# Attention scores with low parts of the keys stored twice, all matmuls over 128 rows

## The chip, the cores and the metric

The kernel runs on one core of a Trainium2 chip. The metric is the time of one execution on the device, in microseconds (us). TensorE (PE) multiplies matrices, VectorE (DVE), ScalarE (ACT) and GpSimd (POOL) work on tiles in the on-chip memory, and SyncE (SP) issues the DMA transfers, one after the other in a fixed order.

## The reference

Two transformer-like blocks over 1024 tokens of 1024 features, all in float32; the first block has two layers, each an attention mixer and a convolutional gated feed-forward. Only the mixer matters here. It runs four groups of four heads and adds their projections:

```python
o_a = neighbourhood_attention_2d(a_q, a_k, a_v, na_rpb[l])     # A: a window of 8 x 16 grid points, with a bias
o_b = dense_attention_blocked(q_b, k_b, v_b, 96 ** -0.5)       # B: latent keys, 96 wide
o_c = dense_attention_blocked(q_c, k_c, c_v, 64 ** -0.5)       # C: two key heads for four query heads
o_d = sliding_window_sink_attention(q_d, k_d, d_v, sink, ...)  # D: +-128 tokens, two key heads
mixed = jnp.concatenate([o_a, o_b, o_c, o_d], axis=-1) @ w_out[l]
```

In A, C and D a score is the product of a query and a key of 64 elements.

## The kernel before

Float32 accuracy is had from float32r matmuls: every operand x is split into h (rounded to float32r) and l = x - h, and a product is h\*h + h\*l + l\*h. For the heads of 64 elements the three products are packed into two matmuls, in `fused` (L561 to L564): the query tile holds h in one half of its 128 rows and l in the other, the tile kh holds the keys' h twice below each other, so that the first matmul (L563) gives h\*h + l\*h; the second (L564) adds h\*l from the 64 rows that hold the query's h, against a tile kl that holds the low parts of two key heads below each other.

```python
nc.tensor.matmul(ps, lhsT=q, rhs=kh, start=True, stop=False)
nc.tensor.matmul(ps, lhsT=q[b], rhs=kl[b], start=False, stop=True)
```

For the first key head of a pair q is [h; l], for the second [l; h], since h must stand in the rows of that head's kl. Three attentions use `fused`:

- C (`c_scores`): 4 heads x 8 query tiles, blocks of 1024 keys, two 512-column pairs each. Its queries (`cqs`), keys (`ckh`) and low parts (`ckl`) are laid into tiles by DMA moves (`cq_dests`, `k_dests`) that SP issues before the attention.
- D (`d_block`): 4 heads x 8 tiles, one pair of 256 or 384 columns. Operands were spilled to memory (`dq_dests`, `k_dests`) and are loaded again (`dq`, `dk`); the mask `dmask` is added.
- A (`a_block_of`): 2 pairs of heads x 8 tiles, one pair of 512 columns or of 512 and 128. `a_qk` spills its operands, `a_load` loads 5 operand tiles for a pair of heads, and two bias images a head: 896 columns for the first and last two query tiles, 640 for the four in the middle.

After a block's scores come a row maximum on VectorE (L555, L585 or L616), the exponential on ScalarE (L557, L587, L618), transposes on TensorE (L510), their split (L515 to L517) and the products with the values (L533, L527).

Projections (`a_qk`, `a_v`, `d_q`, `b_latent` and others) run beside the attentions as a queue of steps (`Feed`); six steps of it come ahead of C. A planner reorders the instructions of each engine from the program's order when the kernel is built, by estimated costs; the buffers of a tag are taken in program order (`fifo`). The tag q has 10 buffers of [128, 1024], which hold all operands above and the biases; the tag pj has 8 of [128, 512]. In PSUM the tag A, which takes the scores, has two buffers of 1024 columns. A move is one DMA (`move`, L350); a weight is loaded by L210 and split by L241 and L242.

Of the kernel before, what the change touches and what calls it, by code (L numbers as in the profile page):

```python
# [50 lines left out]
# spilled operands of the first block's attention: tiles of [128, 1024]  # L51
P_DQ, P_DK, P_AV, P_A, P_BV, P_KPE, P_N = 0, 4, 7, 11, 21, 25, 26


def run(gen):
    """runs a generator to its end and returns what it returns"""
    while True:
        try:
            next(gen)
        except StopIteration as e:  # L60
            return e.value
# [5 lines left out]
class Feed:  # L67
    """work in steps, to be emitted between the steps of other work"""
# [29 lines left out]
class Net:  # L98
# [39 lines left out]
    def fifo(self):  # L138
        """buffers of a tag are taken in program order"""
# [18 lines left out]
    def t(self, tag, dt=F32):  # L158
        """a buffer of a tag: [128, 1024] or [128, 512]"""
# [6 lines left out]
    def ps(self, tag):  # L166
        """A: two banks; T, O, J: one bank"""
# [26 lines left out]
    # ---- weights: load a 128 x n image, split it into two float32r parts  # L194
# [3 lines left out]
    def weights(self, srcs, n):  # L198
        """images beside each other, n columns in all"""
# [17 lines left out]
    def weight_x(self, src, k):  # L217
        """a weight image of k x 512 columns, split into buffers of the tag x"""
# [10 lines left out]
    def mm3(self, ps, terms, first=True, last=True):  # L229
        """terms: ((stationary h, l), (moving h, l)) pairs summed into ps"""  # L230
# [7 lines left out]
    def split(self, full, h, l, eng=None):  # L238
        """h = float32r(full), l = full - h"""
# [22 lines left out]
    def mean_sq(self, tiles, width, tag="v", fast=False):  # L262
        """mean over the features (partitions of all tiles) of the squares, on every partition; fast: no sums on VectorE, the first few on GpSimd"""
# [26 lines left out]
    # ---- x (8 tiles of [128 features, 512 tokens]) -> split normalised x  # L290
# [32 lines left out]
    # ---- x_new = x_old + rms(y) * gain, in y's place  # L323
# [14 lines left out]
    # ---- feature-major projection of a weight tile, half by half  # L338
# [13 lines left out]
    # ================================================================ mixing  # L352
    def mix(self, l, xs, src, dst):
# [16 lines left out]
        # ---- rotary embedding of two tiles that hold the halves of every head  # L370
# [39 lines left out]
        # query heads as [h; l] for the first key head and [l; h] for the second  # L410
        def cq_dests(ah, al, bh, bl):
            for h in range(4):
                r = slice(32 * h, 32 * h + 32)
                for k, s in enumerate((ah, bh, al, bl) if h < 2 else (al, bl, ah, bh)):
                    self.move(cqs[h][32 * k:32 * k + 32], s[r])

        def dq_dests(ah, al, bh, bl):
            for h in range(4):
                r = slice(32 * h, 32 * h + 32)
                for k, s in enumerate((ah, bh, al, bl) if h < 2 else (al, bl, ah, bh)):  # L420
                    self.move(PR[P_DQ + h, 32 * k:32 * k + 32], s[r])

        def k_dests(ah, al, bh, bl):
            for h in range(2):
                for k, (sh, so) in enumerate(((ah, al), (bh, bl))):
                    c, d = slice(32 * h, 32 * h + 32), slice(64 + 32 * h, 96 + 32 * h)
                    r = slice(64 * h + 32 * k, 64 * h + 32 * k + 32)
                    for r0 in (32 * k, 64 + 32 * k):
                        self.move(ckh[h][r0:r0 + 32], sh[c])
                        self.move(PR[P_DK + h, r0:r0 + 32], sh[d])  # L430
                    self.move(ckl[r], so[c])
                    self.move(PR[P_DK + 2, r], so[d])

        # ---- token-major values of 128 tokens: [128, 4 heads x (h | l)], h,l for even heads and l,h for odd
# [24 lines left out]
        # ---- attention  # L459
        def combine(o, s, chunk, q0, narrow):  # L460
            direct = chunk in (0, 3)
            """rows of the even head: h part + l part; of the odd head: l part + h part; over the sums"""
# [24 lines left out]
        def products(o, e, V, vh, P, s, chunk, qq):  # L487
            """adds the products of the values with the transposed exponentials of some query tiles"""
# [51 lines left out]
        def attend(pair, quarters, block, V, vh, chunk):  # L540
            """block(e, head, query tile, sum) -> (exponentials [128, keys], first key tile, number of key tiles)"""
# [19 lines left out]
        def fused(ps, q, b, kh, kl):  # L561
            """q = [h; l] or [l; h], kh twice below each other, kl in the rows b of q's h"""
            nc.tensor.matmul(ps, lhsT=q, rhs=kh, start=True, stop=False)  # L563
            nc.tensor.matmul(ps, lhsT=q[b], rhs=kl[b], start=False, stop=True)  # L564
# [3 lines left out]
        def c_scores(ps, h, q0):  # L568
            for c in (slice(0, 512), slice(512, 1024)):
                fused(ps[:, c], cqs[h][:, q0:q0 + 128], rows(h // 2), ckh[h // 2][:, c], ckl[:, c])  # L570

        def d_block(e, h, i, s):
# [6 lines left out]
            fused(ps, dq[h][:, i * 128:i * 128 + 128], rows(h // 2), dk[h // 2][:, kc], dk[2][:, kc])  # L579
# [10 lines left out]
        def a_load(n):  # L590
            """operands and biases of a pair of neighbourhood heads"""
            ops = [load(P_A + 5 * n + k) for k in range(5)]
            G = []
            for e in range(2):
                g, gm = self.t("q"), self.t("q")
# [1212 lines left out]
```

## Time and profile before

| | |
|---|---|
| median of 3 runs | 3912.29 us (3910.96 to 3913.23) |
| profiled execution, span from first to last instruction | 3919.4 us |
| TensorE matmuls, busy | 3678.4 us (94%), 17088 matmuls |
| VectorE, busy | 2399.7 us (61%) |
| ScalarE, busy | 1614.8 us (41%) |
| GpSimd, busy | 1576.9 us (40%) |
| mean granted clock of TensorE | 0.967 |

The profile is of one execution, another than the three runs; the page gives its span and no separate time for it. Times inside the trace count from the first instruction. TensorE's matmuls overlap (a row's duration goes on while the next has started), so its pace is read from the distance of starts. In the forms of TensorE's rows, "64\*128" is a stationary operand of 64 rows and 128 columns and "64x512" the moving one. "issue" as a releaser means that the profile shows nothing that the engine waited for. SPq rows are DMA issues by SP. A row of busy time by stretch gives the stretch and its length, then the busy time and, in brackets, the instructions of PE, PEld (weight loads), DVE, ACT and POOL, then the granted clock, the DMA share and GB/s.

### The profile page before, as it was taken

The page shows a single profiled execution, that of the slowest core. Times are in us where ns is not written, and L with a number is a line of the kernel's source. Part 1 is how long each engine was busy: PE and PEld are TensorE (multiplying, and loading weights), DVE is VectorE, ACT ScalarE, POOL GpSimd, SP SyncE. Part 2 cuts the span into 40 slices and gives each one's busy share as a digit, 9 for nine tenths or more (in the row PEclk, how much of TensorE's full clock was granted, in tenths as well). Part 3 has the DMA queues.
Part 4 walks back from the last instruction along what each step waited for, and adds up shares of the span by engine and source line. Part 5 has one row for each costly group of instructions (what it writes and reads, how often), then busy time and mean ns, then how long its engine had stood idle before and what let it go on. Part 6 is the DMA issues. An engine that isn't in the chain of part 4 may idle for free. (4 is left out here: it accounts for less than half of the span.)

```text
span 3919.4 us, 46844 instructions
## 1 busy us (share of the span) xinstructions
PE 3678.4 (94%) x17088; PEld 2936.3 (75%) x17088; DVE 2399.7 (61%) x3218; ACT 1614.8 (41%) x2802; POOL 1576.9 (40%) x1176
## 2 busy tenths in 40 slices
PE   6999999899999998999999979999999889897998
PEld 5777678678888885767677858888887668776776
DVE  6465865865564437556775784344534878686547
ACT  4344755433222233345665544234443433324333
POOL 4344433632222224534533463222323454545444
PEclk9999999899999998999999989999999989998999
DMA  3532553322222113343364432111111311111114
GB/s 105 144 105 98 177 170 133 104 100 84 78 81 84 49 57 116 92 120 121 105 204 126 137 108 68 62 54 52 62 60 60 113 49 54 43 49 38 52 52 142
DMA packets 201752, 362.99 MB, mean 93 GB/s; under 512 B 26289, under 2 KB 49073, under 8 KB 201521
## 3 DMA queue, kind: packets, MB, share of 16 engines
q1 hardware_dynamic: 201520, 360.00, 29.0%
q8 instruction: 134, 2.20, 0.2%
q14 instruction: 98, 0.79, 0.1%
HBM read 268.14 MB, written 73.93 MB: 87 GB/s over the span
## 5 line engine op out<-in xcount | busy, mean ns | idle before, releaser
L242 POOL TENSOR_TENSOR wlZ<-wrZ,whZ 128x512 fp32r<-128x512 f32 x584 | 823.7, 1428 | 1512.1 <-ACT whZ L241 1431.1
L235 PE MATMUL AZ<-xZ,whZ 128*128 128x512 f32 x4096 | 1280.7, 393 | 32.4 <-DVE pZ L1416 13.0
L235 PEld LDWEIGHTS AZ<-xZ,whZ 128*128 128x128 f32 x4096 | 773.2, 189 | 203.0 <-issue 18.2
L235 PE MATMUL AZ<-xZ,wlZ 128*128 128x512 f32 x2048 | 803.2, 392 | 3.8 <-POOL wlZ L242 3.4
L241 ACT CAST whZ<-wrZ 128x512 fp32r<-128x512 f32 x584 | 335.2, 613 | 959.5 <-issue 343.6
L235 PEld LDWEIGHTS AZ<-xZ,wlZ 128*128 128x128 f32 x2048 | 387.5, 189 | 88.0 <-POOL wlZ L242 6.0
L980 DVE SCALAR_TENSOR_TENSOR vZ<-AZ,pv,vZ 128x1023 f32<-128x1023 f32 x168 | 215.1, 1280 | 342.7 <-ACT vZ L975 340.2
L517 POOL TENSOR_TENSOR ptZ<-pfZ,ptZ 128x512 fp32r<-128x512 f32 (+1 forms) x200 | 263.9, 1320 | 347.6 <-DVE ptZ L516 316.2
L235 PE MATMUL JZ<-xZ,whZ 128*128 128x512 f32 (+1 forms) x1120 | 369.7, 406 | 33.8 <-DVE xZ L242 7.8
L515 ACT COPY pfZ<-TZ 128x512 f32<-128x512 f32 (+2 forms) x400 | 219.7, 557 | 261.2 <-PE TZ L510 168.8
L235 PE MATMUL TZ<-qZ,whZ 128*128 128x512 f32 x856 | 266.9, 393 | 22.3 <-DVE pjZ L1365 14.9
L533 PE MATMUL OZ<-ptZ,vZ 128*128 128x256 f32 (+1 forms) x1344 | 262.2, 310 | 23.5 <-POOL ptZ L517 11.2
L516 DVE CAST ptZ<-pfZ 128x512 fp32r<-128x512 f32 (+2 forms) x400 | 206.2, 520 | 125.0 <-ACT pfZ L515 120.2
L235 PEld LDWEIGHTS JZ<-xZ,whZ 128*128 128x128 f32 (+1 forms) x1120 | 203.7, 189 | 87.4 <-issue 10.2
L510 PE MATMUL TZ<-ident,pZ 128*128 128x128 f32 x1488 | 243.4, 285 | 18.5 <-ACT pfZ L515 12.6
L533 PEld LDWEIGHTS OZ<-ptZ,vZ 128*128 128x128 f32 x1344 | 201.2, 198 | 48.0 <-POOL ptZ L517 14.1
L235 PE MATMUL JZ<-xZ,wlZ 128*128 128x512 f32 (+1 forms) x560 | 223.7, 399 | 0.9 <-POOL wlZ L242 0.9
L510 PEld LDWEIGHTS TZ<-ident,pZ 128*128 128x128 f32 x1488 | 179.5, 145 | 50.7 <-ACT pfZ L515 18.7
L555 DVE TENSOR_REDUCE s1Z<-AZ 128x1 f32<-128x1024 f32 x128 | 156.3, 1222 | 89.8 <-PE AZ L564 48.3
L235 PEld LDWEIGHTS TZ<-qZ,whZ 128*128 128x128 f32 x856 | 161.7, 190 | 58.5 <-issue 15.7
L1392 DVE SCALAR_TENSOR_TENSOR vZ<-qZ,pv,vZ 128x1009 f32<-128x1009 f32 (+14 forms) x120 | 193.4, 1630 | 4.1 <-ACT vZ L1382 2.4
L235 PE MATMUL TZ<-qZ,wlZ 128*128 128x512 f32 x428 | 167.8, 394 | 0.0
(434 smaller groups left out, 6213.0 us busy)
## 6 DMA issues: line engine op xcount, KB each, us to landing
wrZ<-wup SPq DMA_DIRECT2D x184, 256.0 KB, 2.8
wrZ<-wi SPq DMA_DIRECT2D x156, 256.0 KB, 2.8
wrZ<-wdn SPq DMA_DIRECT2D x112, 256.0 KB, 2.8
qZ<-sc_pr SPq DMA_DIRECT2D x34, 512.0 KB, 4.4
wrZ<-wo SPq DMA_DIRECT2D x64, 256.0 KB, 2.8
sc_ot<-cbZ SPq DMA_DIRECT2D x56, 256.0 KB, 2.5
xZ<-sc_ot SPq DMA_DIRECT2D x56, 256.0 KB, 5.4
wrZ<-modw SPq DMA_DIRECT2D x48, 256.0 KB, 2.8
```

Of the source, the lines that this page charges most:

```text
L235: self.nc.tensor.matmul(ps, lhsT=a, rhs=b, start=first and k == 0, stop=last and k == n - 1)
L241: nc.scalar.copy(h, full)
L242: (eng or nc.vector).tensor_tensor(out=l, in0=full, in1=h.bitcast(F32), op=ALU.subtract)
L510: nc.tensor.transpose(ps[:, n:n + 128], blk, self.ident)
L515: nc.scalar.copy(pf[:, 0:n], ps[:, 0:n])
L516: nc.vector.tensor_copy(ph[:, 0:n], pf[:, 0:n])
L517: (nc.gpsimd if SHARE[self.turn2 % len(SHARE)] else nc.vector).tensor_tensor(out=pl[:, 0:n], in0=pf[:, 0:n], in1=ph[:, 0:n].bitcast(F32), ...
L533: nc.tensor.matmul(o[:, c0:c0 + w], lhsT=v, rhs=x[:, at[k]:at[k] + w], start=(k == order[0] and x is ph), stop=(k == order[-1] and x is pl ...
L555: nc.vector.tensor_reduce(out=nmx, in_=ps, axis=AX.X, op=ALU.max, negate=True)
L980: nc.vector.scalar_tensor_tensor(out=o, in0=i, scalar=w, in1=o, op0=ALU.mult, op1=ALU.add)
L1392: nc.vector.scalar_tensor_tensor(out=o, in0=i, scalar=w[k], in1=o, op0=ALU.mult, op1=ALU.add)
```

## The change

The low parts of the keys get a tile for each key head, in which they stand twice below each other like the high parts; the query tile is [h; l] for every head; the second matmul takes all 128 rows, and so also adds l\*l. The spilled operands grow (`P_DK` 3 to 4 tiles, `P_A` 5 to 6 for a pair of heads). `k_dests` makes 32 moves instead of 24, `a_qk` 8 instead of 5 for each half of a key projection. The bias of A is loaded in three parts of 640 columns: for the first two query tiles, for the middle four, and, when query tile 2 of the first head comes, for the last two. The mask of D goes from a q buffer to a pj buffer. Comments and texts in the functions were taken out as well.

```diff
-P_DQ, P_DK, P_AV, P_A, P_BV, P_KPE, P_N = 0, 4, 7, 11, 21, 25, 26
+P_DQ, P_DK, P_AV, P_A, P_BV, P_KPE, P_N = 0, 4, 8, 12, 24, 28, 29
...
-                for k, s in enumerate((ah, bh, al, bl) if h < 2 else (al, bl, ah, bh)):
+                for k, s in enumerate((ah, bh, al, bl)):
...
         def k_dests(ah, al, bh, bl):
-            for h in range(2):
-                for k, (sh, so) in enumerate(((ah, al), (bh, bl))):
-                    c, d = slice(32 * h, 32 * h + 32), slice(64 + 32 * h, 96 + 32 * h)
-                    r = slice(64 * h + 32 * k, 64 * h + 32 * k + 32)
-                    for r0 in (32 * k, 64 + 32 * k):
-                        self.move(ckh[h][r0:r0 + 32], sh[c])
-                        self.move(PR[P_DK + h, r0:r0 + 32], sh[d])
-                    self.move(ckl[r], so[c])
-                    self.move(PR[P_DK + 2, r], so[d])
+            for part, (tiles, pr, srcs) in enumerate(((ckh, P_DK, (ah, bh)), (ckl, P_DK + 2, (al, bl)))):
+                for h in range(2):
+                    for k, src in enumerate(srcs):
+                        for r0 in (32 * k, 64 + 32 * k):
+                            self.move(tiles[h][r0:r0 + 32], src[32 * h:32 * h + 32])
+                            self.move(PR[pr + h, r0:r0 + 32], src[64 + 32 * h:96 + 32 * h])
...
-        def fused(ps, q, b, kh, kl):
+        def fused(ps, q, kh, kl):
             nc.tensor.matmul(ps, lhsT=q, rhs=kh, start=True, stop=False)
-            nc.tensor.matmul(ps, lhsT=q[b], rhs=kl[b], start=False, stop=True)
+            nc.tensor.matmul(ps, lhsT=q, rhs=kl, start=False, stop=True)
...
-                fused(ps[:, c], cqs[h][:, q0:q0 + 128], rows(h // 2), ckh[h // 2][:, c], ckl[:, c])
+                fused(ps[:, c], cqs[h][:, q0:q0 + 128], ckh[h // 2][:, c], ckl[h // 2][:, c])
...
-            ops = [load(P_A + 5 * n + k) for k in range(5)]
-            G = []
-            for e in range(2):
-                g, gm = self.t("q"), self.t("q")
-                nc.sync.dma_start(g[:, 0:896], I["rpbx"][l, 2 * n + e, :, 0:896])
-                nc.sync.dma_start(gm[:, 0:640], I["rpbx"][l, 2 * n + e, :, 896:1536])
-                G.append((g, gm))
-            return ops, G
+            ops = [load(P_A + 6 * n + k) for k in range(6)]
+            G = {}
+
+            def bias(part):
+                for e in range(2):
+                    G[part, e] = self.t("q")
+                    c = (256, 896, 0)[part]
+                    nc.sync.dma_start(G[part, e][:, 0:640], I["rpbx"][l, 2 * n + e, :, c:c + 640])
+
+            bias(0)
+            bias(1)
+            return ops, G, bias
...
             def a_block(e, h, i, s):
                 nk, k0 = NA_NK[i] * 128, NA_KS[i] * 64
+                if i == 2 and e == 0:
+                    load_bias(2)
...
                         for e in range(2):
                             for r in range(2):
-                                self.move(PR[P_A + 5 * n + 2 + e, rows(r), sl], h[rows(e)])
-                        self.move(PR[P_A + 5 * n + 4, :, sl], lo)
+                                self.move(PR[P_A + 6 * n + 2 + e, rows(r), sl], h[rows(e)])
+                                self.move(PR[P_A + 6 * n + 4 + e, rows(r), sl], lo[rows(e)])
...
-        ckl = self.t("q", F32R)
+        ckl = [self.t("q", F32R) for _ in range(2)]
...
-        dmask = self.t("q")[:, 0:384]
+        dmask = self.t("pj")[:, 0:384]
...
-        dk = [load(P_DK + h) for h in range(3)]
+        dk = [load(P_DK + h) for h in range(4)]
```

## Rows read from the trace of the kernel before

**Rows 1.** Busy time by stretch: C, D, A of layer one; both layers' sum.
```profile
150.00:332.00 182.00, 178.44 (x962) 135.31 (x961) 113.88 (x164) 88.23 (x170) 71.84 (x56) 0.98 0.38 115
332.00:432.00 100.00, 94.49 (x520) 68.69 (x520) 72.61 (x168) 60.32 (x153) 52.75 (x68) 0.97 0.32 104
432.00:532.00 100.00, 95.94 (x490) 70.34 (x489) 76.16 (x183) 62.98 (x148) 38.03 (x35) 0.92 0.63 196
...
sum 751.00, PE 725.03 PEld 540.38 DVE 522.26 ACT 421.04 POOL 323.89; mean PE 120.84 PEld 90.06 DVE 87.04 ACT 70.17 POOL 53.98
```
**Rows 2.** Waits of VectorE, 150 to 332 us: total, times, longest.
```profile
DVE s1Z L555 <- PE AZ L564: 23.9, 21, 2.7
```

**Rows 3.** Busy time by stretch, around the end of D.
```profile
400.00:450.00 50.00, 44.39 (x228) 29.26 (x227) 45.55 (x106) 37.34 (x94) 30.98 (x35) 0.93 0.41 133
```

**Rows 4.** Timeline of TensorE's matmuls in C: start, duration, line, forms, count.
```profile
200.47 0.40 PE L563 MATMUL AZ<-qZ,qZ 128*128 128x512 f32 x1
200.79 0.50 PE L564 MATMUL AZ<-qZ,qZ 64*128 64x512 f32 x1
201.22 0.50 PE L563 MATMUL AZ<-qZ,qZ 128*128 128x512 f32 x1
...
202.08 0.33 PE L510 MATMUL TZ<-ident,pZ 128*128 128x128 f32 x1
...
204.55 0.62 PE L235 MATMUL JZ<-xZ,whZ 128*128 128x512 f32 x2
205.01 0.40 PE L235 MATMUL JZ<-xZ,wlZ 128*128 128x512 f32 x1
```

**Rows 5.** Line L564: instructions, and idle time of its engine before them.
```profile
L564 PE MATMUL AZ<-qZ,qZ x288: 322/492/792, 150.7 to 2054.2; 64*128 64x512 f32 x110, 64*128 64x384 f32 x22, 64*128 64x256 f32 x12
...
  issue: 59.6, 239
```

**Rows 6.** Timeline of TensorE's matmuls in attention B.
```profile
559.16 1.55 PE L235 MATMUL AZ<-xZ,qZ 96*128 96x512 f32 x6
560.54 0.52 PE L533 MATMUL OZ<-ptZ,vZ 128*128 128x256 f32 x3
```

**Rows 7.** Timeline of TensorE in D: two pairs, between the first and last row.
```profile
385.54 0.42 PE L563 MATMUL AZ<-qZ,qZ 128*128 128x384 f32 x1
...
387.00 0.57 PE L527 MATMUL OZ<-ptZ,vZ 128*64 128x128 f32 x6
```

**Rows 8.** Timeline of TensorE in D, where one pair is interleaved.
```profile
352.82 0.34 PE L563 MATMUL AZ<-qZ,qZ 128*128 128x384 f32 x1
353.00 0.49 PE L510 MATMUL TZ<-ident,pZ 128*128 128x128 f32 x3
...
354.26 0.44 PE L564 MATMUL AZ<-qZ,qZ 64*128 64x384 f32 x2
354.63 0.50 PE L235 MATMUL JZ<-xZ,whZ 128*128 128x512 f32 x1
```

**Rows 9.** Timeline of TensorE in A: transposes, then a block of 640 columns.
```profile
452.15 0.66 PE L510 MATMUL TZ<-ident,pZ 128*128 128x128 f32 x4
452.57 0.37 PE L533 MATMUL OZ<-ptZ,vZ 128*128 128x256 f32 x1
...
454.18 0.47 PE L563 MATMUL AZ<-qZ,qZ 128*128 128x512 f32 x1
...
455.52 0.50 PE L563 MATMUL AZ<-qZ,qZ 128*128 128x512 f32 x1
```

**Rows 10.** Busy time by stretch, in the first 15 us of C.
```profile
161.00:164.00 3.00, 3.00 (x8) 1.45 (x6) 1.12 (x2) 2.28 (x4) 1.28 (x1) 0.50 0.89 230
```

**Rows 11.** Timeline of TensorE at the start of C; idle time and releaser in brackets.
```profile
158.49 0.44 PE L510 MATMUL TZ<-ident,pZ 128*128 128x128 f32 x2 [1.83 <-ACT pZ L557]
```

**Rows 12.** Timeline of SP's DMA issues at the start of C, layer one.
```profile
136.71 0.54 SPq L350 DMA_DIRECT2D qZ<-qZ  x1
...
151.01 15.11 SPq L350 DMA_DIRECT2D sc_pr<-pjZ  x22
166.17 1.55 SPq L210 DMA_DIRECT2D wrZ<-wi  x3
```

**Rows 13.** Timeline of ScalarE at the start of C, layer one.
```profile
154.74 0.60 ACT L653 ACTIVATE pjZ<-TZ 128x512 fp32r<-128x512 f32 x1 [9.02 <-DMA sc_pr<-pjZ]
```

**Rows 14.** Timeline of ScalarE at the start of C, layer two.
```profile
1683.78 0.60 ACT L653 ACTIVATE pjZ<-TZ 128x512 fp32r<-128x512 f32 x1 [10.01 <-DMA sc_pr<-pjZ]
```

More of the change, by code (lines that the diff above doesn't have):

```diff
@@ L419, in dq_dests @@
                 r = slice(32 * h, 32 * h + 32)
-                for k, s in enumerate((ah, bh, al, bl) if h < 2 else (al, bl, ah, bh)):
+                for k, s in enumerate((ah, bh, al, bl)):
                     self.move(PR[P_DQ + h, 32 * k:32 * k + 32], s[r])
         def k_dests(ah, al, bh, bl):
-            for h in range(2):
-                for k, (sh, so) in enumerate(((ah, al), (bh, bl))):
-                    c, d = slice(32 * h, 32 * h + 32), slice(64 + 32 * h, 96 + 32 * h)
-                    r = slice(64 * h + 32 * k, 64 * h + 32 * k + 32)
-                    for r0 in (32 * k, 64 + 32 * k):
-                        self.move(ckh[h][r0:r0 + 32], sh[c])
-                        self.move(PR[P_DK + h, r0:r0 + 32], sh[d])
-                    self.move(ckl[r], so[c])
-                    self.move(PR[P_DK + 2, r], so[d])
+            for part, (tiles, pr, srcs) in enumerate(((ckh, P_DK, (ah, bh)), (ckl, P_DK + 2, (al, bl)))):
[4 more added lines that the diff above has]
+                            self.move(PR[pr + h, r0:r0 + 32], src[64 + 32 * h:96 + 32 * h])
         def v_tile(ps, dst):
@@ L578, in d_block @@
             kc = slice(k0 * 128, k0 * 128 + n)
-            fused(ps, dq[h][:, i * 128:i * 128 + 128], rows(h // 2), dk[h // 2][:, kc], dk[2][:, kc])
+            fused(ps, dq[h][:, i * 128:i * 128 + 128], dk[h // 2][:, kc], dk[2 + h // 2][:, kc])
             sink = self.nsink[:, l * 4 + h:l * 4 + h + 1]
@@ L590, in a_load, with a_block_of @@
         def a_load(n):
-            ops = [load(P_A + 5 * n + k) for k in range(5)]
-            G = []
-            for e in range(2):
-                g, gm = self.t("q"), self.t("q")
-                nc.sync.dma_start(g[:, 0:896], I["rpbx"][l, 2 * n + e, :, 0:896])
-                nc.sync.dma_start(gm[:, 0:640], I["rpbx"][l, 2 * n + e, :, 896:1536])
-                G.append((g, gm))
-            return ops, G
-        def a_block_of(ops, G):
+            ops = [load(P_A + 6 * n + k) for k in range(6)]
[8 more added lines that the diff above has]
+            return ops, G, bias
+        def a_block_of(ops, G, load_bias):
             def a_block(e, h, i, s):
                 nk, k0 = NA_NK[i] * 128, NA_KS[i] * 64
+                if i == 2 and e == 0:
+                    load_bias(2)
                 ps = self.ps("A")
@@ L606, in a_block @@
                     c1 = min(nk, c0 + 512)
-                    fused(ps[:, c0:c1], ops[e][:, i * 128:i * 128 + 128], rows(e),
-                          ops[2 + e][:, k0 + c0:k0 + c1], ops[4][:, k0 + c0:k0 + c1])
-                if 2 <= i <= 5:
-                    bias = G[e][1][:, 0:640]
-                else:
-                    o = (NA_KS[i] - 2 * i + 6) * 64
-                    bias = G[e][0][:, o:o + nk]
+                    fused(ps[:, c0:c1], ops[e][:, i * 128:i * 128 + 128],
+                          ops[2 + e][:, k0 + c0:k0 + c1], ops[4 + e][:, k0 + c0:k0 + c1])
+                part = 0 if i < 2 else 1 if i < 6 else 2
+                o = 0 if part == 1 else (NA_KS[i] - 2 * i + 6) * 64 - (256, 0, 0)[part]
+                bias = G[part, e][:, o:o + nk]
                 p = self.t("p")
@@ L654, in a_qk @@
                         nc.vector.scalar_tensor_tensor(out=lo, in0=ps, scalar=sc, in1=h.bitcast(F32), op0=ALU.mult, op1=ALU.subtract)
-                        for e, hl in enumerate(((h, lo), (lo, h))):
-                            for r in range(2):
-                                self.move(PR[P_A + 5 * n + e, rows(r), sl], hl[r][rows(e)])
+                        for e in range(2):
+                            for r, t in enumerate((h, lo)):
+                                self.move(PR[P_A + 6 * n + e, rows(r), sl], t[rows(e)])
                     yield
@@ L937, in mix @@
         for n in range(2):
-            ops, G = a_load(n)
-            feed.beside(attend((2 * n, 2 * n + 1), range(4), a_block_of(ops, G), Va, lambda e, n=n: 2 * n + e, 1 + n), 8, PLAN[2][n])
+            ops, G, bias = a_load(n)
+            feed.beside(attend((2 * n, 2 * n + 1), range(4), a_block_of(ops, G, bias), Va, lambda e, n=n: 2 * n + e, 1 + n), 8, PLAN[2][n])
         feed.drain()
```

## The prediction

> **What bounds the kernel now.** I read the granted clock and the busy time of the attention stretches first, then the order and spacing of the matmuls inside them, then who waits for whom, and last the queue of DMA issues (SP), because the change adds transfers to it.
>
> The stretches in which the changed lines run are three per layer: attention C (150 to 332 us in the first layer), D (332 to 432) and A (432 to 532). TensorE is busy 94 to 98% of each; over both layers it is busy 725 of 751 us and the next engine, VectorE, 522 [rows 1]. In C the reader is to see that VectorE's row reduction L555 waits 23.9 us in total for the second score matmul L564 [rows 2]: the scores are late, not their readers. So C is TensorE's. D and A are less clear: VectorE is busy 73 and 76 of 100 us there [rows 1], and in the 50 us around the change from D to A it reaches 45.55 while TensorE falls to 44.39 [rows 3]. Where VectorE stands at nine tenths, a faster TensorE will wait for it.
>
> But a busy TensorE is not one at its best pace. A 128-row, 512-column matmul follows its like after 0.23 us (two take 204.55 to 205.01) [rows 4]. In the score pairs the step from the 128-row L563 to the 64-row L564 is 0.32 us for the first of a block and 0.43 us for the later ones, and the step out of L564 is 0.43 us [rows 4]. The weight load of L564 sat idle 59.6 us in 239 of 288 cases with no releaser but "issue" [rows 5]. It is not ordinary accumulation that does this, nor a row count below 128: six matmuls of 96 rows run from 559.16 to 560.54, 0.23 us each, three and three into a bank [rows 6]. What differs is the form 64\*128, so each L564 costs a wait on entry and one on exit.
>
> **The change, step by step.**
>
> (1) *The second score matmul with 128 rows.* It removes no instruction: 288 matmuls and loads stay [rows 5]. It takes the 64\*128 form away, so I price every step at that of a 128-row matmul of the same columns.
> C: a block of two 512-column pairs takes 200.47 to 202.08 = 1.61 us [rows 4]; four steps of 0.23 are 0.92; saved 0.69. 32 blocks a layer, 64 in all: 44 us.
> D: two 384-column pairs take 385.54 to 387.00 = 1.46 us [rows 7]; a 128-row 384-column matmul lets the next start after 0.18 (352.82 to 353.00) [rows 8], so 4 x 0.18 = 0.72; saved 0.37 a pair. 32 pairs a layer (a quarter have 256 columns; I take them alike): 64 x 0.37 = 24 us, less some 2 because the products L527 that often follow have a 128\*64 form of their own: 22 us.
> A: a block of 512 + 128 columns takes 454.18 to 455.52 = 1.34 us [rows 9]; without the form 2 x 0.23 + 2 x 0.11 (the 128-column L510 of rows 9: four from 452.15 to 452.57) = 0.68; saved 0.66. Half of the 32 blocks of a layer are such, half have one 512-column pair (0.35, half of C's block): 32 x 0.66 + 32 x 0.35 = 32 us.
> Sum at full clock: 44 + 22 + 32 = 98 us of TensorE's time. The bound below is nothing (if other engines set the pace), the bound above 98 and some 8 more, since pairs that ran at half clock (0.50 in 161 to 164) [rows 10] lose about twice as much.
>
> How much of it reaches the end: in C TensorE's waits are one of 1.83 us [rows 11] and crumbs, so nine tenths: 40 us. In D the stage would shrink from 100 to 89 us with VectorE at 73; I take four fifths, 18 us. In A it would shrink to 84 with VectorE at 76, as tight as the stretch of rows 3; I take seven tenths, 23 us. Together 81 us.
>
> One row speaks for the 64-row form: once a layer two L564 of D start together at 354.26, and the next matmul follows at 354.63 [rows 8]; nowhere else do two L564 stand next to each other. The Trainium skill, TensorE: Matmul & The Clock Gate (Part 3, Packing small matmuls) and TensorEngine Tiling (Array Packing) (Performance Considerations), makes that a rule against this change: matmuls of short contraction in different row groups run side by side, so that a 64-row one is the cheaper. By the rule the second products would lose by the change (the last rival gives the time, 3945); by rows 4, 7 and 9 they gain the 98 us, and the trace bears the rule out for that one pair a layer only.
>
> (2) *More moves on SP at the start of C.* The keys' moves (k_dests) grow from 24 to 32. SP issues 24 from 136.71 to 151.01, 0.60 us each [rows 12], so 8 more are 4.8 us. Queued behind them are the 22 spills of a_qk from 151.01 and the weight loads of 166.17 [rows 12]. ScalarE waits 9.02 us at its L653 for the first of these spills to free a buffer (until 154.74), and 10.01 us in the second layer [rows 13, 14]; behind it on ScalarE stand the exponentials, behind L654 on VectorE the first reduction. That is the wait of 1.83 us that TensorE shows at 158.49 [rows 11]. Moving the spills back by 4.8 us moves this chain by as much: 4.8 us a layer, 9.6 in all, and nothing covers it once the two score buffers of PSUM (tag A) are full. A longer idle stretch may also lengthen the stretch at half clock behind it (rows 10): up to 3.4 us a layer, I take 2. Together 14 us. Bounds: nothing (if the order of TensorE's work is refilled with projections), 25 us (if all 12 added spills, below, add to it).
>
> (3) *a_qk*: 3 more moves for each key half, 12 a layer at 0.69 us (22 in 15.1 us) [rows 12] = 8 us of SP's time. The weight loads that now start at 166.17 come 4.8 + 6 x 0.69 = 9 us later. TensorE has the attention itself to do until then; I take nothing and keep 8 us a layer for the range.
>
> (4) *Loads.* One more dk and one more operand of each pair of A; D holds 8 of the 10 buffers as before (the mask leaves for pj), A 10 instead of 9. The first three tiles that D frees are now what A's first head needs (operands, then the bias of its first two query tiles), and the biases of the last tiles come while the middle ones run: nothing either way, 3 us a boundary for the range. The mask takes one of eight pj buffers during D, which the projections beside D use; it is part of why D gets only four fifths.
>
> **Sum**: -81 + 14 = -67 us. It is made against the profiled execution, whose span of 3919.4 us lies 7 us above the median of the runs, 3912.3; the difference is carried over: 3912.3 - 67 = 3845.
>
> **The rivals.**
> *All of it arrives*: the planner fills every gap and the queue's delay is covered. For it: projections run ahead of their place all through C. Against it: rows 3. 3912 - 98 - 4 (half-clock pairs) = 3810.
> *The attention's chain takes over in D and A*: VectorE and ScalarE set the pace, only C gains. For it: rows 3; against: TensorE's few waits in A. 3912 - 40 - 8 + 20 (queue at the upper half) = 3884.
> *The SP queue becomes the bound, slower*: place: the first 40 us of C. The 20 added moves and spills (4.8 + 8 = 13 us a layer) all stand in front of the weights, and TensorE idles that long and runs at half clock after it: 2 x (13 + 7) = 40 us. It decides once less than 40 of the 98 us arrive. For it: the 9 to 10 us waits of rows 13 and 14; against: 40 us are C's alone. At 25 us arriving: 3927.
> *Packing was worth more than the form costs*: if 64-row products shared their time as the pair of rows 8 does, a change that ends it would lose 288 x 0.115 = 33 us: 3945. Against it: that pair is the only one of 144 a layer, and two 128-row products of 0.18 take no more than its 0.37. This is the rule of the two pages of the Trainium skill named above.
>
> **How the numbers follow.** The forecast 0.62 (3825 to 3865); all arrives 0.18; chain takes over 0.14; SP queue 0.04; packing 0.02. The range reaches to the first two rivals: 3803 to 3886. About 0.2% (8 us) is what a measurement of this kernel can tell from no change. Faster 0.94, the same 0.02, slower 0.04.
>
> **What would show it.** Right: all score matmuls in one form, 0.23 us from start to start, the idle of L564's weight load gone, C shorter by some 17 us a layer, L653's first wait longer by 4 to 5 us. Wrong: steps above 0.3 us although the form is 128\*128 (then it was the repeated stationary or the shared bank); C shorter by less than 10 us; or D and A unchanged with VectorE above 90%.

## The result

| | before | after |
|---|---|---|
| median of the runs | 3912.76 us (4 runs, 3910.96 to 3924.01) | 3850.56 us (4 runs, 3844.90 to 3855.97) |
| span of the profiled execution | 3919.4 us | 3854.2 us |

The ratio is 0.9839, with a 95% interval from 0.9820 to 0.9857: the change takes 62 us off. Forecast were 3845 us and 3803 to 3886; the time lies 6 us above the forecast. Both profiled executions lie some microseconds above their medians; their spans differ by 65.2 us.

**Where the time went.** Busy time by stretch of the kernel after, C, D and A of each layer; the columns are the stretch, its length, the busy time of TensorE, its weight loads, VectorE, ScalarE and GpSimd (with instructions), and the mean granted clock, the DMA share and GB/s:

```profile
150.00:304.00 154.00, 145.75 (x920) 127.90 (x919) 112.07 (x162) 86.85 (x166) 69.07 (x54) 0.99 0.51 143
307.00:407.00 100.00, 89.78 (x546) 71.63 (x545) 68.91 (x164) 60.68 (x154) 51.66 (x70) 1.00 0.34 113
407.00:500.00 93.00, 80.00 (x492) 66.07 (x493) 80.48 (x191) 64.23 (x152) 41.42 (x36) 0.96 0.69 218
...
sum 694.00, PE 631.78 PEld 532.73 DVE 523.20 ACT 423.66 POOL 324.79; mean PE 105.30 PEld 88.79 DVE 87.20 ACT 70.61 POOL 54.13
```

Against [rows 1] TensorE's busy time falls by 93 us (725.03 to 631.78) while VectorE's stays (522.26 and 523.20). C is 28 us shorter in this cut, D is not, A is 7 us shorter. In A TensorE and VectorE are now level at 80 of 93 us: neither is full.

The pairs at their new pace: timeline of TensorE's matmuls after, a block of C, a pair of D between transposes and products, and a pair of A (start, duration, line, forms, count); L562 and L563 are the L563 and L564 of before:

```profile
164.92 0.39 PE L562 MATMUL AZ<-qZ,qZ 128*128 128x512 f32 x1
165.16 0.40 PE L563 MATMUL AZ<-qZ,qZ 128*128 128x512 f32 x1
165.39 0.39 PE L562 MATMUL AZ<-qZ,qZ 128*128 128x512 f32 x1
165.62 0.40 PE L563 MATMUL AZ<-qZ,qZ 128*128 128x512 f32 x1
165.85 0.64 PE L532 MATMUL OZ<-ptZ,vZ 128*128 128x256 f32 x4
...
370.61 0.34 PE L562 MATMUL AZ<-qZ,qZ 128*128 128x384 f32 x1
370.79 0.33 PE L563 MATMUL AZ<-qZ,qZ 128*128 128x384 f32 x1
370.96 0.98 PE L526 MATMUL OZ<-ptZ,vZ 128*64 128x256 f32 x10
...
440.22 0.48 PE L562 MATMUL AZ<-qZ,qZ 128*128 128x512 f32 x1
440.54 0.40 PE L563 MATMUL AZ<-qZ,qZ 128*128 128x512 f32 x1
440.77 0.52 PE L235 MATMUL JZ<-xZ,xZ 128*128 128x256 f32 x3
```

A block of C takes 164.92 to 165.85 = 0.93 us, where [rows 4] have 1.61; a 384-column pair of D 0.35 us. In A the first matmul of this pair, behind a transpose, still takes 0.32 us; the second takes 0.23. The weight loads of the second matmul hardly wait any more. What line L563 of after waited for:

```profile
L563 PE MATMUL AZ<-qZ,qZ x288: 272/393/628, 152.2 to 1994.5; 128*128 128x512 f32 x111, 128*128 128x384 f32 x22, 128*128 128x256 f32 x11
...
  issue: 4.6, 4
```

"Issue" is 4.6 us in 4 cases, against 59.6 in 239 [rows 5].

**Time by stage and kernel.** The lengths below are worked out from the trace: C from the first start of its row reduction (L555 before, L554 after) to the last end, D from there to A's first reader of scores, A to the first reduction of attention B; both layers added. "Projections in C, D" counts the matmuls of the work beside the attention in the first layer; "idle" is TensorE's idle time over C, D and A of both layers, from the start of C as defined here. e12 is the kernel after once more. Ratios are to the kernel before, run on the same chip.

| kernel | C | D | A | idle | projections in C, D | median us | ratio, 95% interval |
|---|---|---|---|---|---|---|---|
| before | 347.8 | 205.9 | 194.3 | 26 | 374, 150 | 3912.76 | |
| after | 304.2 | 207.6 | 185.2 | 62 | 353, 176 | 3850.56 | 0.9839, 0.9820 to 0.9857 |
| e1_form_only | 313.3 | 196.6 | 176.0 | 55 | 372, 150 | 3853.11 | 0.9844, 0.9831 to 0.9856 |
| e2_moves_only | 340.0 | 222.8 | 207.6 | 32 | 357, 177 | 3929.26 | 1.0046, 1.0034 to 1.0058 |
| e3_only_c | 303.2 | 224.3 | 205.4 | 41 | 353, 176 | 3893.65 | 0.9948, 0.9936 to 0.9960 |
| e4_only_da | 346.8 | 203.6 | 183.6 | 50 | 358, 176 | 3895.78 | 0.9946, 0.9934 to 0.9958 |
| e5_grouped | 327.9 | 206.1 | 180.7 | 34 | 372, 150 | 3889.09 | 0.9932, 0.9915 to 0.9949 |
| e6_mask_own | 302.9 | 212.0 | 180.9 | 61 | 353, 176 | 3858.92 | 0.9859, 0.9844 to 0.9874 |
| e7_late_spill | 319.9 | 194.7 | 175.5 | 55 | 394, 130 | 3887.40 | 0.9934, 0.9921 to 0.9947 |
| e8_zero_rows | 307.3 | 198.0 | 177.0 | 55 | 372, 152 | 3848.23 | 0.9832, 0.9818 to 0.9845 |
| e9_a_pool | 303.9 | 206.5 | 190.2 | 62 | 353, 176 | 3858.20 | 0.9863, 0.9840 to 0.9886 |
| e10_d_dve | 304.4 | 206.1 | 184.1 | 56 | 353, 176 | 3849.62 | 0.9842, 0.9824 to 0.9861 |
| e11_zero_dve | 305.3 | 198.3 | 181.0 | 55 | 372, 152 | 3854.66 | 0.9849, 0.9835 to 0.9864 |
| e12_after_same_chip | 304.1 | 207.5 | 185.9 | 62 | 353, 176 | 3854.84 | 0.9848, 0.9834 to 0.9861 |

From before to after C gives 43.6 us, D takes 1.7, A gives 9.1; together 51 of the 65 us between the spans. The other 14 lie outside these stages (C of layer one begins 2.8 us earlier, the rest is in the attentions B and the feed-forward parts); some 6 of them are projections that now run inside C, D and A (the count of their time there rises from 239.5 to 245.9 us).

### The profile page after: what moved, and what is told of

Same layout as the page of the kernel before. It is cut to its first block, busy times and chain, and to the rows that moved or that the text cites. A ratio compares the mean times of both kernels' runs of the same rounds, so it can differ in the third digit from the quotient of the medians.

```text
span 3854.2 us, 46916 instructions
## 1 busy us (share of the span) xinstructions
PE 3579.7 (93%) x17088; PEld 2921.9 (76%) x17088; DVE 2406.4 (62%) x3218; ACT 1616.9 (42%) x2802; POOL 1574.2 (41%) x1176
## 5 line engine op out<-in xcount | busy, mean ns | idle before, releaser
L235 PE MATMUL AZ<-xZ,whZ 128*128 128x512 f32 x4096 | 1279.6, 393 | 34.4 <-DVE pZ L1419 13.6
L235 PEld LDWEIGHTS AZ<-xZ,whZ 128*128 128x128 f32 x4096 | 772.1, 189 | 205.4 <-issue 19.4
L235 PE MATMUL AZ<-xZ,wlZ 128*128 128x512 f32 x2048 | 802.7, 392 | 3.8 <-POOL wlZ L242 3.4
L235 PEld LDWEIGHTS AZ<-xZ,wlZ 128*128 128x128 f32 x2048 | 387.1, 189 | 87.5 <-POOL wlZ L242 6.2
L235 PE MATMUL JZ<-xZ,whZ 128*128 128x512 f32 (+1 forms) x1120 | 369.8, 405 | 35.9 <-DVE xZ L242 7.9
L515 DVE CAST ptZ<-pfZ 128x512 fp32r<-128x512 f32 (+2 forms) x400 | 222.3, 558 | 105.8 <-ACT pfZ L514 90.8
L235 PE MATMUL TZ<-qZ,whZ 128*128 128x512 f32 x856 | 266.5, 393 | 19.0 <-DVE pjZ L1368 11.7
L235 PEld LDWEIGHTS JZ<-xZ,whZ 128*128 128x128 f32 (+1 forms) x1120 | 203.9, 189 | 86.2 <-DVE xZ L242 8.8
L509 PE MATMUL TZ<-ident,pZ 128*128 128x128 f32 x1488 | 242.5, 282 | 21.0 <-ACT pfZ L514 12.2
L235 PE MATMUL JZ<-xZ,wlZ 128*128 128x512 f32 (+1 forms) x560 | 223.5, 399 | 0.0
L235 PEld LDWEIGHTS TZ<-qZ,whZ 128*128 128x128 f32 x856 | 161.2, 189 | 55.6 <-issue 9.7
L554 DVE TENSOR_REDUCE s1Z<-AZ 128x1 f32<-128x1024 f32 x128 | 155.9, 1221 | 65.8 <-PE AZ L235 34.6
L556 ACT ACTIVATE pZ<-AZ,s1Z 128x1024 f32<-128x1024 f32 x128 | 143.5, 1122 | 62.5 <-DVE s1Z L554 33.5
```

Of the source, the lines that this page charges most:

```text
L235: self.nc.tensor.matmul(ps, lhsT=a, rhs=b, start=first and k == 0, stop=last and k == n - 1)
L509: nc.tensor.transpose(ps[:, n:n + 128], blk, self.ident)
L515: nc.vector.tensor_copy(ph[:, 0:n], pf[:, 0:n])
L554: nc.vector.tensor_reduce(out=nmx, in_=ps, axis=AX.X, op=ALU.max, negate=True)
L556: nc.scalar.activation(p, ps, AF.Exp, bias=nmx, scale=1.0, accum_out=s)
```

## The experiments

**The form alone: e1.** The kernel before, with its second matmul over all 128 rows of the stacked low-part tile.

```diff
-            nc.tensor.matmul(ps, lhsT=q[b], rhs=kl[b], start=False, stop=True)
+            nc.tensor.matmul(ps, lhsT=q, rhs=kl, start=False, stop=True)
```

> The kernel before with one edit: the second score matmul takes all 128 rows of the same operands (its sums are then other numbers, since the tile of low parts holds two key heads). No transfer, no buffer, no bias load is changed. Theory T1 (as predicted: the new form gains some 81 us and the added moves at the start of C give back 14): 3912 - 80 = about 3832, 15 to 20 us faster than the changed kernel. Rival T2 (the planner covers the added moves, because the first exponential now runs ahead of the waiting ScalarE instruction; what is lost of the 98 us is lost in the attention's own chain): within 6 us of the changed kernel, about 3850, with D again about as long as before.

Measured 3853.11 us, 0.9844: the form alone does what the whole change does, and the intervals overlap almost wholly. Beside the new form the added moves have no price that can be told from zero (by the two intervals, within some 9 us), so T1's 14 us is out. T2's time came, its clause on D did not: with the form alone D is 9.3 us shorter than before. Against after, D and A are 11 and 9 us shorter, C is 9 us longer (the table). What e1 adds to the sum by the way is the low part of a query times the low part of another head's key, a product of two low parts like l\*l; so one line of the change brings all of its time.

**The moves alone: e2.** The kernel after, with the 64-row second matmul.

```diff
-            nc.tensor.matmul(ps, lhsT=q, rhs=kl, start=False, stop=True)
+            nc.tensor.matmul(ps, lhsT=q[0:64], rhs=kl[0:64], start=False, stop=True)
```

> The changed kernel with all its moves, loads and buffers, but the second score matmul on rows 0 to 63 alone (h of the query, low parts of the keys: the sum of the kernel before). T1: the added moves show alone: 3912 + 10 to 14 = about 3924. T2: within 5 us of the kernel before, 3907 to 3917. Both: starts of score pairs 0.43 us apart again.

Measured 3929.26 us, 1.0046: with the old form the moves and loads do have a price, 13 to 23 us, the size of step (2), but not in its place. C is 7.8 us shorter; D and A are 16.9 and 13.3 us longer. Projections L235 by stretch show why for D; first the kernel before, then e2 (columns: stretch, length, busy time and count of TensorE and its loads for this line alone):

```profile
156.00:330.00 174.00, 46.16 (x185) 32.91 (x185) 0.98 0.35 110
332.00:435.00 103.00, 34.72 (x135) 21.39 (x134) 0.97 0.34 111
```

```profile
151.00:320.00 169.00, 42.01 (x163) 28.97 (x163) 1.00 0.45 128
320.00:432.00 112.00, 44.57 (x174) 28.73 (x174) 0.94 0.32 105
```

C has 22 fewer of them and D more (39 by these cuts, of which that of e2 is 9 us longer). By the bounds of the stage table it is 17 fewer in C and 27 more in D; C begins 4.8 us earlier in e2 (151.2 against 156.0), so part of the 27 comes from before C. Work that waited for its turn moved on, and D ran at a lower clock, 0.94 against 0.97. What makes A longer in e2 I could not tie to one wait.

**C alone, D and A alone: e3 and e4.** The 128-row form in C with 64 rows in D and A (e3), and the other way round (e4); the moves stay in both.

```diff
+        def fused(ps, q, kh, kl, n):
...
+            nc.tensor.matmul(ps, lhsT=q[0:n], rhs=kl[0:n], start=False, stop=True)
```

> The changed kernel with the 128-row second matmul in C alone; D and A take 64 rows. If C carries the gain as its stretch suggests (22.6 and 21 us shorter in the changed kernel): 3912 - 45 = about 3867. If the gain of C was work pushed into D (26 projection matmuls, 7 us a layer, ran in D instead of C): about 3880, with D longer than 105 us. T1's sum gives 3912 - 40 + 14 = 3886.

> The changed kernel with the 128-row second matmul in D and A alone; C takes 64 rows. If D gains nothing by itself (its chain bounds it) and A some 5 us a layer: 3912 - 10 = about 3902. If D's gain was only hidden by the projections that came over from C: D shorter by 8 or more us a layer and the time about 3880.

Measured 0.9948 and 0.9946. Against e2 (1.0046) C's form is worth 0.98% = 38 us and that of D and A together 1.00% = 39 us; both at once (after) 2.07% = 81 us, or 1.98% by e12. The two add up: nothing that one gains is taken from the other. e3's 3893.65 us lies above all three figures expected of it, e4's 3895.78 between its two: both fit moves that keep a price where the old form stays. With the moves the form is worth some 80 us, without them (e1) 60.

**Is it the change of form? e5.** The kernel before, but both 128-row matmuls of a block come first, then both 64-row ones: the same instructions with half the changes of form, in all blocks with two pairs.

```diff
+            for p, h, l in zip(ps, kh, kl):
+                nc.tensor.matmul(p, lhsT=q, rhs=h, start=True, stop=False)
+            for p, h, l in zip(ps, kh, kl):
+                nc.tensor.matmul(p, lhsT=q[b], rhs=l[b], start=False, stop=True)
```

> The kernel before with another order inside a block of scores: where a block has two pairs, both 128-row matmuls first, then both 64-row ones, so that the form changes twice in a block instead of four times. Nothing else differs. Theory F (the cost lies at the change of form): the second 64-row matmul starts 0.23 us after the first, a block of C takes about 1.2 us instead of 1.61, 64 blocks of C and 32 of A save 38 us of TensorE's time, of which some 22 arrive: about 3890. Rival W (a 64-row matmul is slow by itself): starts still 0.43 us apart, no change, 3912.

Measured 3889.09 us, 0.9932: Theory F's time, and Rival W fails. Timeline of TensorE in e5: a block of C by single matmuls, then a stretch where pairs of the two forms follow each other; L564 is the 128-row matmul, L566 the 64-row one:

```profile
199.85 0.39 PE L564 MATMUL AZ<-qZ,qZ 128*128 128x512 f32 x1
200.08 0.39 PE L564 MATMUL AZ<-qZ,qZ 128*128 128x512 f32 x1
200.40 0.49 PE L566 MATMUL AZ<-qZ,qZ 64*128 64x512 f32 x1
200.74 0.39 PE L566 MATMUL AZ<-qZ,qZ 64*128 64x512 f32 x1
201.06 0.33 PE L510 MATMUL TZ<-ident,pZ 128*128 128x128 f32 x1
...
208.52 0.73 PE L566 MATMUL AZ<-qZ,qZ 64*128 64x512 f32 x2
209.18 0.73 PE L564 MATMUL AZ<-qZ,qZ 128*128 128x512 f32 x2
209.84 0.73 PE L566 MATMUL AZ<-qZ,qZ 64*128 64x512 f32 x2
210.50 0.50 PE L235 MATMUL JZ<-xZ,whZ 128*128 128x512 f32 x1
210.84 0.39 PE L235 MATMUL JZ<-xZ,wlZ 128*128 128x512 f32 x1
211.07 0.63 PE L235 MATMUL JZ<-xZ,whZ 128*128 128x512 f32 x2
```

The block takes 199.85 to 201.06 = 1.21 us, between the 1.61 of before and the 0.93 of after. But its steps are 0.23, 0.32, 0.34 and 0.32 us: the second 64-row matmul starts 0.34 us after the first, neither at Theory F's 0.23 nor at Rival W's 0.43. The second part shows why. There the two 128-row matmuls between 64-row ones take 0.66 us (209.18 to 209.84), as long as two 64-row ones, and the first 128-row matmul of a projection behind a 64-row one takes 0.34 (210.50 to 210.84), the next 0.23. So a change of form adds some 0.1 us to the step across it and 0.1 us to the step behind it, and the row count adds nothing that shows. Counted over e5's trace at full clock (512 columns, no transpose beside): a step right behind a change has a median of 0.337 us in 28 cases of two 128-row matmuls and in 87 of two 64-row ones, and like 128-row matmuls with no change near step by 0.227. [rows 4] follow from it: 0.32 across a block's first change, 0.43 where each step is across one change and behind another.

A stationary that changes is not the cause: the projection's changes from wlZ (210.84) to whZ (211.07) within 0.23 us. No run has three 64-row matmuls in a row, so their step with no change near is not shown by itself.

**Why D did not shrink: e6, e7, e8.** Three edits of the kernel after. e6 gives the mask a buffer of its own, against the theory that its place among the eight pj buffers holds the projections up.

```diff
-        dmask = self.t("pj")[:, 0:384]
+        dmask = self.sp.tile([128, 384], F32, name=self.nm("dm"), tag="dm", bufs=1)
```

> The changed kernel with D's mask in a buffer of its own instead of a pj buffer (to make room, the tag of one-column tiles has 12 buffers instead of 16). Theory M (D is long because the projections beside it have seven pj buffers instead of eight): D shorter by 4 us or more a layer, about 3842. Rival Q (D is long because projections come over from C, behind SP's queue): D still has some 176 projection matmuls and 102 to 105 us, the time within 4 us of 3851.

Measured 3858.92 us, 0.9859; D is 212.0 us, not shorter than after's 207.6, and still has 176 projections. Theory M's gain did not come; the time lies 8 us above rival Q's too. Since the edit also takes four of the 16 buffers of one-column tiles away, it does not clear the mask's buffer wholly.

e7 takes the 16 spills of D's keys out of the queue's first stretch and issues them behind the six projection steps ahead of C.

```diff
-                            self.move(PR[pr + h, r0:r0 + 32], src[64 + 32 * h:96 + 32 * h])
+                            late.append((PR[pr + h, r0:r0 + 32], src[64 + 32 * h:96 + 32 * h]))
...
+        for d, s in late:
+            self.move(d, s)
```

> The changed kernel with the 16 spills of D's keys issued after the six steps of projections that come ahead of C instead of before them; the moves that C itself needs keep their place. Theory Q: ScalarE's wait at the start of C (until 159.2 in the changed kernel) ends some 9 us earlier, weights come earlier, D has about 150 projection matmuls instead of 176 and is 98 to 100 us long, C keeps its length or grows by up to 5: about 3843. Rival M: no change, 3851.

Measured 3887.40 us, 0.9934: 37 us worse than after, for another reason than its theory was about. D is 194.7 us with 130 projections, as expected, but C begins later. SP's queue and TensorE's timeline at the start of C in e7:

```profile
136.08 4.98 SPq L350 DMA_DIRECT2D qZ<-qZ  x8
141.10 17.89 SPq L350 DMA_DIRECT2D sc_pr<-pjZ  x28
159.04 5.15 SPq L350 DMA_DIRECT2D sc_pr<-qZ  x9
164.80 4.99 SPq L350 DMA_DIRECT2D qZ<-qZ  x8
```

```profile
169.15 0.76 PE L565 MATMUL AZ<-qZ,qZ 128*128 128x512 f32 x1 [16.08 <-DMA qZ<-qZ]
```

The moves of C's own low parts (the second group of qZ<-qZ) go out at 164.80, behind nine of the deferred spills, and TensorE stands idle for 16.08 us until one lands. C's first reduction comes at 170.8 us instead of 153.2. This is the rival "the SP queue becomes the bound", produced by hand: it needed the score operands themselves behind the spills.

e8 fills the lower halves of the low-part tiles with zeros (GpSimd) in place of the second copy, so that 16 of the 20 added moves per layer go and the low loads are half as large; it leaves the small l\*l term out, as the kernel before does.

```diff
-                        for r0 in (32 * k, 64 + 32 * k):
+                        for r0 in (32 * k, 64 + 32 * k)[:2 - part]:
...
+        zero = lambda t: nc.gpsimd.memset(t[64:128].bitcast(F32), 0.0)
```

> The changed kernel with zeros instead of the second copy of the low parts (rows 64 to 127 of these tiles are set to zero on GpSimd; the sum is that of the kernel before, without the low-by-low term). The moves of the keys fall back from 32 to 24, those of a key projection from 8 to 6, and the low tiles' loads are half as large; 10 zero fillings a layer come onto GpSimd. Theory Q: as with the late spills, fewer projections in D, about 3843, and the wait at the start of C 4 to 5 us shorter. Rival M: within 4 us of 3851. If the fillings are in GpSimd's way at the start of C or A: slower than 3856.

Measured 3848.23 us, 0.9832: rival M's time, with the projections in D (152) of Theory Q. The fillings are 8 a layer, not 10, of about 1 us. D is 9.6 and A 8.2 us shorter than after, C 3.1 longer, but the total is that of after within the intervals: the span is 6.5 us shorter, the rest is given back outside of these stages. Projections L235 in C and D of layer one, by the bounds of the stage table, in e8 (e1 has the same 180 and 144):

```profile
156.00:309.60 153.60, 45.62 (x180) 32.57 (x180) 0.98 0.41 124
309.60:408.20 98.60, 36.51 (x144) 23.69 (x144) 0.98 0.34 110
```

With few or no added moves 180 of them run in C and 144 in D, with all of them 165 and 171 (e2) or 161 and 170 (after): the moves push projections from C into D, in either form. Each costs its time in one stage or in another, which is one reason why the stages trade places.

**What bounds A and D now: e9, e10.** SHARE deals the subtractions of the split out between VectorE and GpSimd. e9 gives all of A's to GpSimd, e10 all of D's to VectorE.

```diff
-                (nc.gpsimd if SHARE[self.turn2 % len(SHARE)] else nc.vector).tensor_tensor(
+                (nc.gpsimd if chunk in (1, 2) or SHARE[self.turn2 % len(SHARE)] else nc.vector).tensor_tensor(
```

> The changed kernel with all subtractions of the split of A's exponentials on GpSimd (20 more a layer there, at 1.3 us; VectorE has 15 us a layer less to do in A). Theory V (VectorE, at 80 of 93 us, sets A's pace and makes the 11 to 12 us of TensorE's idle time a layer): A shorter by 5 us or more a layer, about 3840. Rival L (the idle time is latency: each step of the chain from scores to products waits for the one before, on whichever engine it is): a longer subtraction makes the chain longer, A the same or longer by up to 6 us a layer, 3850 to 3862.

> The changed kernel with all subtractions of the split of D's exponentials on VectorE (0.65 us each instead of 1.0 to 1.3 on GpSimd; VectorE's 69 of 100 us in D become about 80). Theory L (latency of the chain makes the 9 to 12 us of idle time in D): D shorter by 2 to 5 us a layer, about 3844. Theory V (VectorE sets the pace): D longer, about 3858.

Measured 3858.20 us, 0.9863, and 3849.62 us, 0.9842. Busy time of A, layer one, in e9 (columns as above), then two lines of VectorE there (instructions, busy time, mean ns of one, idle time before them), first of after and then of e9:

```profile
409.00:501.00 92.00, 78.39 (x499) 65.20 (x497) 77.00 (x170) 64.84 (x154) 62.46 (x54) 0.98 0.68 217
```

```profile
L515 DVE CAST ptZ<-pfZ 128x512 fp32r<-128x512 f32 (+2 forms) x42 | 21.2, 505 | 4.8 <-ACT pfZ L514 2.9 <-POOL ptZ L516 1.4
L516 DVE TENSOR_TENSOR ptZ<-pfZ,ptZ 128x512 fp32r<-128x512 f32 (+2 forms) x21 | 14.6, 696 | 0.5
...
L515 DVE CAST ptZ<-pfZ 128x512 fp32r<-128x512 f32 (+2 forms) x42 | 27.7, 663 | 4.8 <-ACT pfZ L514 4.4
L516 DVE TENSOR_TENSOR ptZ<-pfZ,ptZ 128x128 fp32r<-128x128 f32 (+1 forms) x3 | 1.9, 628 | 0.1
```

GpSimd rises to 62 us and A is 92.3 and 97.9 us long, after 91.6 and 93.6: rival L's time. But the edit did not relieve VectorE by the 15 us that were meant. Its subtractions fell from 21 to 3, while its casts, the same 42, went from 505 to 663 ns beside the busier GpSimd; its busy time in A fell by 1.4 us (78.4 to 77.0) in layer one and 5.8 in layer two. So e9 does not decide between V and L. In D e10 gives VectorE the subtractions and its busy time stays too (73.0 and 69.6 us, then 72.3 and 72.6), while GpSimd's falls from 54 to 37. TensorE's idle time in D goes from 11.2 and 8.9 to 8.5 and 6.5 us, D gets 3.1 us shorter in one layer and 1.6 longer in the other, and the total does not follow: neither theory's time came.

**Both small gains together: e11, and after once more: e12.**

```diff
+        zero = lambda t: nc.gpsimd.memset(t[64:128].bitcast(F32), 0.0)
...
+                (nc.gpsimd if chunk not in (6, 7) and SHARE[self.turn2 % len(SHARE)] else nc.vector).tensor_tensor(
```

> The two edits that shortened D one at a time, zeros in place of the second copy of the low parts and D's subtractions all on VectorE, put together. Theory S (the stages trade work: what D saves is mostly projections that stay in C, and the sum is TensorE's work plus its waits): 3845 +-4 us, D 98 us a layer, C some 2.5 us longer than in the changed kernel, and within 0.2% of the changed kernel itself when both run on one chip. Theory G (the two gains add up and arrive): 3838 us or less, 0.3% under the changed kernel.

> The changed kernel again, nothing edited, on the chip of the combined version, so that the two can be compared: 3850 +-4 us by both theories.

Measured 3854.66 us and, for the kernel after on the same chip, 3854.84 us: 0.9849 and 0.9848. Theory S holds against after on the same chip (its 3845 does not: that chip reads 4 us more for after as well); Theory G fails. The gains do not add up, and no version that I ran is shown to beat the change as it was made.

## Why the prediction was right, and where its terms were off

**What bounds the kernel: right.** TensorE's own time was what C, D and A were made of, and the price was that of the form. e5 shows that it lies at the change of form, e1 that the form alone yields the gain. That each L564 costs "a wait on entry and one on exit" is nearly it: each change, in or out, lengthens the step across it and the one behind it by 0.1 us each.

**Step (1), the saving of TensorE's time: right in size.** Summed from the starts of the score matmuls in the trace, less TensorE's idle: C goes from 99.6 to 61.6 us in both layers, D from 46.8 to 26.8, A from 70.2 to 41.3. That is 38, 20 and 29 us; with some 4 us of pairs that ran ahead of C's first reduction 91 us, where 44, 22 and 32 were forecast (98). What stands in neither sum is the step behind a block, which loses another 0.1 us with the change. The 0.69 a block of C was taken from one block; the mean is 0.65 (four times 49.8 us over 121 matmuls before less 30.8 over 124 after, in layer one).

**How much of it arrives: off, in D and A.** The forecast was 40, 18 and 23 = 81 us. e1, where only the form changes, shows the stages getting shorter by 34.5, 9.3 and 18.3 us: 62. The missing part is TensorE's idle, 26 us before, 55 in e1 and 62 after. It is what the rival "the attention's chain takes over in D and A" said, but in part only, and with VectorE busy some 69% of D and 87% of A, not full. Waits of TensorE after, in D and then in A of layer one (who waits for whom, total, times, longest):

```profile
PE AZ L562 <- DVE s1Z L584: 4.0, 4, 1.7
PE OZ L526 <- DVE ptZ L515: 2.2, 3, 1.3
...
PE OZ L526 <- POOL ptZ L516: 1.3, 1, 1.3
```

```profile
PE TZ L509 <- ACT pfZ L514: 3.6, 8, 0.7
PE JZ L235 <- DVE pjZ L760: 2.0, 2, 1.5
PE AZ L562 <- DVE s1Z L619: 1.7, 1, 1.7
PE OZ L532 <- DVE ptZ L516: 1.5, 2, 1.1
```

The idle time is spread over short waits, and most of them end with VectorE: 9.4 of the 11.6 us listed for D (307 to 412) and 6.5 of the 12.2 for A (409 to 501). Whether VectorE's work sets the pace or the length of the chain from scores to product, with few blocks of scores under way at once, stays open: e9 and e10 changed VectorE's busy time too little to tell, and a version with more score buffers was not tried.

**Step (2), the queue: right at its place, wrong in what follows.** SP, then ScalarE, then TensorE at the start of C after, by their timelines:

```profile
154.92 0.58 SPq L350 DMA_DIRECT2D sc_pr<-qZ  x1
155.54 18.87 SPq L350 DMA_DIRECT2D sc_pr<-pjZ  x28
174.45 8.47 SPq L210 DMA_DIRECT2D wrZ<-wi  x5
```

```profile
154.41 1.12 ACT L556 ACTIVATE pZ<-AZ,s1Z 128x1024 f32<-128x1024 f32 x1 [8.98 <-DVE s1Z L554]
...
159.20 0.60 ACT L656 ACTIVATE pjZ<-TZ 128x512 fp32r<-128x512 f32 x1 [3.58 <-DMA sc_pr<-pjZ]
```

```profile
160.69 1.80 PE L509 MATMUL TZ<-ident,pZ 128*128 128x128 f32 x7 [2.86 <-DVE pjZ L657]
```

The same wait of TensorE in e1, which has none of the added moves:

```profile
158.05 0.47 PE L510 MATMUL TZ<-ident,pZ 128*128 128x128 f32 x1 [3.37 <-ACT pZ L557]
```

The spills start at 155.54 instead of 151.01, and the wait of L656 (the L653 of before) ends at 159.20 instead of 154.74 [rows 12, 13]: 4.5 us later, as forecast (4 to 5). The weight loads come 8.3 us later (forecast 9). But an exponential now stands ahead of that wait, and TensorE's wait is 2.86 us instead of 1.83 [rows 11], no longer than the 3.37 of e1. So the chain did not move by 4.8 us; C's first reduction comes at 153.2 us, earlier than the 156.0 of before. The failed clause is "nothing covers it once the two score buffers of PSUM (tag A) are full": the order of ScalarE's work was refilled, where the step had thought only of TensorE's order, and of that as its lower bound. The term was -14 us of gain and is about 0 beside the new form (e1 against after). With the old form the moves do cost 18 us (e2), with projections that slip into D and a longer A. Why the price vanishes with the new form stays open; that TensorE then has idle time in D and A to take the slipped work is the likeliest reading, not a shown one.

**Steps (3) and (4): nothing, as forecast, in sum.** e6 gives the clause on the mask no support; e8 shows that the moves shift projections between C and D, which no step had foreseen: D is the one stage that came out as long as before, though 11 us shorter was expected and 26 projections more (7 us) stand in it.

**The sum.** -81 + 14 = -67 was made of two terms that were both too large: e1's stages give -62 and the moves about 0. The errors, 19 and 14 us, largely cancelled. That the forecast was close is in part luck.

**The other rivals.** "All of it arrives" (3810) fails: there are 36 us of new idle time. "Packing" (3945) fails: the 64-row form costs and does not pay. "The SP queue becomes the bound" (3927) fails too, and e7 shows what it takes. The Trainium skill, TensorEngine Tiling (Array Packing) (Tiling Modes), states that changing the tiling mode drains TensorE, with no price; the steps of [rows 4] and of e5 agree with it, and put the price at 0.1 us on the step across a change and 0.1 us on the step behind it.

**What would show it.** One form and 0.23 us steps: yes, but for 0.32 us behind a transpose, so that "steps above 0.3 us" was too wide a sign of being wrong. Weight-load idle gone: 59.6 to 4.6 us. C shorter by some 17 us a layer: 22.6 and 21.0, of which 5 a layer are projections that left it. L653's wait longer by 4 to 5 us: it ends 4.5 us later, but in two parts (8.98 and 3.58 us) with an exponential between.

## What to carry to other kernels

Look at the step from start to start where matmuls of two forms alternate, not at the busy share: if it is longer than that of like matmuls, fill the shorter form up to 128 rows (doubled data, zeros, or rows whose product is small enough to be left in do it alike), or group the forms if that is not to be had; a step of two like matmuls right behind a change still bears half of that change's price. Count on the saved time arriving in full only in the stage where the engine had no second chain close behind, and price the idle that comes instead. Moves in a queue ahead of a planned order may cost nothing at the place where they wait and still shift work by a stage, so read the sum and not one stage.

## What the runs showed of the hardware

The granted clock rose though TensorE idles more. In the cuts of [rows 1] the mean was 0.98, 0.97 and 0.92 of the full 2.4 GHz in C, D and A of layer one, with 94 to 98% of the time busy; after it is 0.99, 1.00 and 0.96, with 86 to 95% busy. Summed from the clock's records in the six stages, the stretches at the 1.2 GHz level fell from 47.8 to 27.2 us. The idle time of a kernel does not tell its time at the lower level here: e2 idles 32 us in these stages and has 54.7 us at 1.2 GHz, after idles 62 and has 27.2.

A change between 64-row and 128-row matmuls of 512 columns costs about 0.2 us, half on the step across it and half on the step behind it, whichever form stands there (e5, counted above). Grouping the forms halves the number of changes, and in C takes TensorE's time for the scores from 99.6 to 77.4 us, where one form takes 61.6; it does not touch the data.

VectorE's casts of the same shape took longer beside more work on GpSimd: the 512-column ones a mean of 478 ns in A of after and 659 in e9, where GpSimd's busy time there is 61 us instead of 40. Moving work from VectorE to GpSimd gave little of VectorE's time back.
